# Two branches' gates and projections with tokens on the result's partitions, their sums transposed, and wide tiles moved by 128 bytes

## The chip, the core and the metric

The kernel runs on one core of one Trainium2 chip. The metric is device time in microseconds, from the first to the last instruction of a launch and what lies around it; lower is better. Before the change the median of three runs is 2205.89 us (2203.31 to 2206.0).

## What is computed

One residual block over 512 tokens of width 2048, in f32. The input is normalised and goes through one wide projection; its columns feed three branches and three merge gates:

```
conv_y = b_gate * conv3(c_gate * u);  o_conv = (conv_y * silu(conv_z)) @ w_conv_out     # 1024 -> 2048
mla_y  = latent attention, 16 heads;  o_mla  = (mla_y  * silu(mla_z))  @ w_mla_out      # 2048 -> 2048
mem_y  = attention to 256 tokens;     o_mem  = (mem_y  * silu(mem_z))  @ w_mem_out      # 1024 -> 2048
merged = sigmoid(g_conv)*o_conv + sigmoid(g_mla)*o_mla + sigmoid(g_mem)*o_mem
out    = x + merged @ w_o                                                               # 2048 -> 2048
```

## The kernel before

**A product of two f32 matrices** is three matmuls: each operand is split into a high part (rounded to float32r, ScalarE, line 122) and a rest (VectorE, line 124), and `mm3` (lines 150 to 155) adds high x high, high x rest and rest x high. Weights come from HBM in chunks of 128 x 1024 values (512 KB) into `raw` tiles, and each chunk is split into `whi` and `wlo` two chunks ahead of its use; there are three such pairs of buffers and ten `raw` tiles, of which the projections' split inputs take six.

**Block groups.** The big products (2048 x 2048 by 512 tokens) are done as a two-by-two block scheme with seven products instead of eight, P1 to P7 (line 913). Each takes a sum or difference of weight blocks (VectorE, `pre`, three chunks ahead) and a sum or difference of token blocks: `00`, `10`, `11`, and the forms T1 to T4, kept split in tiles `blk` (even), `hU` (odd) and `f` (forms), and made for eight pairs of channel blocks by `build` (line 1147) in four steps: sums, evens, forms, odds. The products land in four kinds of banks X, Y, Z, W.

- `block_group` (line 923) gives 512 output channels in 14 chunks. Channels lie on the result's partitions: the weights are the stationary operand, 256 tokens the moving one. A chunk is 24 matmuls 256 wide. It takes one PSUM bank for each of X, Y, Z, W, and groups alternate between the tags `aux` and `acc`, four banks each.
- `block_group_t` (line 1036) gives 1024 channels in 28 chunks with tokens on the result's partitions: token blocks are stationary, 512 weight columns move. A chunk is 12 matmuls 512 wide. It takes two banks for each of X, Y, Z, W, that is all eight. Only the output projection `w_o` (two groups, `out_group`, line 1616) uses it.

A *plain group* (`plain_group`, line 871) is an ordinary product, 24 matmuls 512 wide per chunk. `projection` (line 1474) runs four of them with their gates; before, all in mode F: weights stationary, 512 tokens moving.

**Order of the stages.** Memory keys and values (to 126 us), latent projections, 16 heads of attention with the memory queries' and gates' plain groups between and behind them (to 733 us), then 24 block groups: eight for the convolution's inputs, four for `mla_z`, then four each for the gates of memory, convolution and MLA (`gate_group`, line 1452). The gates go through a sigmoid to `gdram`. Then the memory's projection (16 chunks), multiplied by its gate and stored as first sums to `mdram`; four block groups of the MLA projection (`mla_group`, line 1542), which multiply by the gate, add the sums and store them again; the convolution's projection (16 chunks); and the two output groups.

**The order within.** `drive` (line 794) goes through the planned chunks; at each it emits loads that are due, `pre` and `prep` for later chunks, then small pieces of VectorE's and ScalarE's work (each with a due chunk, a cost and, with `by`, a chunk at which it is emitted in any case) as far as VectorE's room lets them, then the matmuls. Each engine works through its instructions in the order they are emitted. Loads go over SP's queue, stores over ScalarE's, adding transfers over POOL's.

**The junction.** In the convolution's projection a pair p of channel blocks (two blocks of 128) takes these steps, at chunks in the lists of lines 1578 and 1579: its gates are loaded (GATES), its sums are loaded (SUMS, `load_m`, line 1600), the product is multiplied by the gate (TIMES, line 1592), added to the sums (ADDS; for pairs 0 to 3 and 5 by an adding transfer, line 1587, else on VectorE, line 1589), and the four steps of `build` make the token blocks for `w_o` (FORMS). The first output group starts at chunk 16 in the order P1, P7, P5, P6 for each quarter of the pairs.

**Layout.** Wide tiles are allotted in whole multiples of 512 bytes (`Lines`, line 76), on the left side of SBUF from the end of a pool of small tiles, on the right side from the top. A fill of 48 floats (line 49) is in the small pool: with it every wide tile on the left (weights, `raw`, the projections' inputs, the identity) starts 128 bytes past a multiple of 512, and every one on the right (`blk`, `hU`, `f`) at a multiple.

Of the kernel before, what the change touches and what calls it, by code (L numbers as in the profile page):

```python
# [48 lines left out]
SMALL_FILL = 48  # L49
# [45 lines left out]
def body(ctx, tc, a, out):  # L95
# [16 lines left out]
    psum = ctx.enter_context(tc.tile_pool(name="ps", bufs=4, space=bass.MemoryType.PSUM))  # L112
# [3 lines left out]

    def bank(tag):
        return psum.tile([P, 512], F32, tag=tag, name=tag)
# [650 lines left out]


# [90 lines left out]
    tags = [0]  # L861

    def next_banks(n=4, tag=None):
        if tag is not None:
            tags[0] = ("aux", "acc").index(tag)
        else:
            tags[0] += 1
        return [bank("acc" if tags[0] % 2 else "aux") for _ in range(n)]


    def plain_group(src, nch, kc, n, xs, early=4, lead=2, tag=None):
# [4 lines left out]
        for c in range(nch):  # L876
# [13 lines left out]
            def mm(hold=hold, c=c):  # L890
                if c == 0:
                    banks.extend(next_banks(n // P, tag))
                hi, lo = hold["w"]
                for i in range(n // P):
                    for k in range(kc):
                        cols = slice(i * P, (i + 1) * P)
                        mm3(banks[i], (hi[:, k, cols], lo[:, k, cols]), xs(c * kc + k),
# [25 lines left out]
    def block_group(src, tokens, consume, loads=(-8, -7, -3, -2), add=None, halves=False):  # L923
# [70 lines left out]
        for n, ch in HALVES_ORDER if halves else PLAIN_ORDER:  # L994
# [22 lines left out]
                def mm(ch=ch, bn=bn, xn=xn, hold=hold):  # L1017
                    opens = bn not in bk
                    if not bk:
                        tags[0] += 1  # L1020
                        bk["tag"] = "acc" if tags[0] % 2 else "aux"
                    if opens:
                        bk[bn] = bank(bk["tag"])
# [12 lines left out]
    def block_group_t(src, tokens, results, tags_, early=6):  # L1036
# [10 lines left out]
        order = [(name, ch) for ch in range(4) for name in ("P1", "P7", "P5", "P6")]  # L1047
# [3 lines left out]
        for ch in range(4):  # L1051
            for b in range(3):
                when_raw(max(-3, first + max(4 * ch + b // 2 - early, -3 if early < 6 else -9)), 1, None,
                         lambda i=4 * b + ch: load(i))
            when_raw(first + 20 + 2 * ch - 6, 1, None, lambda i=12 + ch: load(i))
# [27 lines left out]
        for name, ch in order:  # L1083
# [21 lines left out]
            def mm(name=name, ch=ch, bn=bn, xn=xn, hold=hold):  # L1105
                opens = bn not in bk
                if opens:
                    bk[bn] = [bank(tags_["XYZW".index(bn)]) for _ in range(2)]
# [13 lines left out]
    def operands(b0, b1, f):  # L1122
        return {"00": (b0[:, 0, :HS], b0[:, 1, :HS]), "T1": (b0[:, 0, HS:], b0[:, 1, HS:]),
                "10": (b1[:, 0, :HS], b1[:, 1, :HS]), "11": (b1[:, 0, HS:], b1[:, 1, HS:]),
# [652 lines left out]
```

## Time and profile before

| | us |
|---|---|
| median of three runs | 2205.89 (2203.31 to 2206.0) |
| profiled execution, its own time | 2205.18 |
| its span, first to last instruction | 2203.4 |
| TensorE busy | 2149.7 |
| VectorE / ScalarE busy | 1575.1 / 1025.8 |
[...]

The span is what the rows below divide up; the profiled execution's own time is 1.8 us more. A matmul's printed duration holds its pipeline, so matmuls overlap; what one costs is the distance between starts.

### The profile page before, as it was taken

Reading aid. Unit: us, or ns where it says so; the run is one execution under the profiler, and the core shown is the slowest. Engines: PE = TensorE matmul, PEld = TensorE weight load, DVE = VectorE, ACT = ScalarE, POOL = GpSimd, SP = SyncE. Lnnn points to the kernel's source line nnn. Section 1 sums busy time; section 2 is a strip of 40 time slices with the busy share of each in tenths; the row PEclk is TensorE's granted clock in tenths of the full one; section 3 lists DMA queues with packets and bytes.
Section 4 is the critical chain, followed back from the end, with each engine's and each line's share of the span. In section 5 each row is a group of like instructions: output and inputs, shape, how many; then the busy total and the mean of one; then the engine's idle time right before and its main releaser. Section 6 shows DMA issues by size and latency. Waiting matters only on the chain.

```text
span 2203.4 us, 35901 instructions
## 1 busy us (share of the span) xinstructions
PE 2149.7 (98%) x14456; PEld 1981.4 (90%) x14456; DVE 1575.1 (71%) x2200; ACT 1025.8 (47%) x1547; POOL 171.8 (8%) x151
## 2 busy tenths in 40 slices
PE   7999999999999999999999999999999999999899
PEld 5788888898778999999999999999999899987787
DVE  7863777774335888787877777777676778857887
ACT  5532667774333444444444444444444443433433
POOL 6510311220001000000000000000000000000000
PEclk9999999999999999999999999999999999999999
DMA  7573212244228523333345334343344764577252
GB/s 260 154 257 107 87 55 67 76 143 147 76 77 258 191 90 106 131 101 124 112 170 185 130 115 149 125 146 125 114 147 149 253 215 164 183 240 253 78 206 91
DMA packets 115255, 322.61 MB, mean 146 GB/s; under 512 B 13200, under 2 KB 13456, under 8 KB 115088
## 3 DMA queue, kind: packets, MB, share of 16 engines
q1 hardware_dynamic: 90000, 274.87, 37.1%
q10 hardware_dynamic: 21600, 38.63, 4.7%
q0 software_dynamic: 3488, 6.82, 1.6%
q8 instruction: 113, 1.85, 0.3%
q14 instruction: 54, 0.44, 0.1%
HBM read 269.41 MB, written 48.23 MB: 144 GB/s over the span
## 4 chain that ended last, share of the span: by engine, by line
PE 68%; issue 2%; DVE 1%; ACT 0%; DMA 0%; POOL 0%; POOLq 0%; DVEq 0%; ACTq 0%
PE aux L155 11%; PE aux L153 11%; PE aux L154 11%; PE acc L154 11%; PE acc L153 11%; PE acc L155 11%; DVE wlo L124 0%; DMA eo<-y 0%; DVE raw L1096 0%; ACT whi L122 0%; DVE y L1592 0%; DVE f L124 0%; PE aux L204 0%; PE aux L1212 0%; DVE blk L124 0%
## 5 line engine op out<-in xcount | busy, mean ns | idle before, releaser
L124 DVE TENSOR_TENSOR wlo<-raw,whi 128x1024 fp32r<-128x1024 f32 x440 | 538.1, 1223 | 377.1 <-ACT whi L122 376.7
L122 ACT ACTIVATE whi<-raw 128x1024 fp32r<-128x1024 f32 x440 | 466.3, 1060 | 704.7 <-PE acc L154 297.6
L1007 DVE TENSOR_TENSOR raw<-raw 128x1024 f32<-128x1024 f32 x168 | 204.6, 1218 | 0.0
L155 PE MATMUL acc<-f,wlo 128*128 128x256 f32 x672 | 189.4, 282 | 0.0
L155 PE MATMUL aux<-f,wlo 128*128 128x256 f32 x672 | 189.4, 282 | 0.0
L154 PE MATMUL aux<-f,whi 128*128 128x256 f32 x672 | 189.3, 282 | 0.0
L154 PE MATMUL acc<-f,whi 128*128 128x256 f32 x672 | 189.3, 282 | 0.0
L153 PE MATMUL acc<-f,whi 128*128 128x256 f32 x672 | 189.1, 281 | 0.0
L153 PE MATMUL aux<-f,whi 128*128 128x256 f32 x672 | 189.1, 281 | 0.0
L147 DVE TENSOR_TENSOR wlo<-raw,whi 128x1024 fp32r<-128x1024 f32 (+3 forms) x97 | 117.7, 1215 | 96.0 <-ACT whi L146 94.7
L153 PE MATMUL acc<-blk,whi 128*128 128x256 f32 (+1 forms) x544 | 165.3, 304 | 9.0 <-ACT sq L1200 9.0
L154 PE MATMUL acc<-blk,whi 128*128 128x256 f32 (+1 forms) x544 | 164.2, 302 | 0.6 <-DVE blk L124 0.6
L154 PE MATMUL acc<-hU,whi 128*128 128x256 f32 (+1 forms) x544 | 164.1, 302 | 0.0
L153 PE MATMUL acc<-hU,whi 128*128 128x256 f32 (+1 forms) x544 | 164.1, 302 | 0.0
L155 PE MATMUL acc<-hU,wlo 128*128 128x256 f32 (+1 forms) x544 | 163.9, 302 | 0.0
L155 PE MATMUL acc<-blk,wlo 128*128 128x256 f32 (+1 forms) x544 | 163.7, 302 | 0.0
L146 ACT ACTIVATE whi<-raw 128x1024 fp32r<-128x1024 f32 (+3 forms) x97 | 92.6, 955 | 124.9 <-PE acc L155 49.2
L155 PE MATMUL aux<-blk,wlo 128*128 128x256 f32 (+1 forms) x480 | 138.9, 289 | 0.0
L155 PE MATMUL aux<-hU,wlo 128*128 128x256 f32 (+1 forms) x480 | 138.9, 289 | 0.0
L154 PE MATMUL aux<-hU,whi 128*128 128x256 f32 (+1 forms) x480 | 138.9, 289 | 0.0
L154 PE MATMUL aux<-blk,whi 128*128 128x256 f32 (+1 forms) x480 | 138.9, 289 | 0.0
L153 PE MATMUL aux<-hU,whi 128*128 128x256 f32 (+1 forms) x480 | 138.7, 289 | 0.0
(379 smaller groups left out, 5820.3 us busy)
## 6 DMA issues: line engine op xcount, KB each, us to landing
raw<-in_w_conv SPq DMA_DIRECT2D x64, 512.0 KB, 4.3
raw<-in_w_mlaz SPq DMA_DIRECT2D x32, 512.0 KB, 4.9
raw<-in_w_gmem SPq DMA_DIRECT2D x32, 512.0 KB, 4.2
raw<-in_w_gconv SPq DMA_DIRECT2D x32, 512.0 KB, 3.9
raw<-in_w_gmla SPq DMA_DIRECT2D x32, 512.0 KB, 3.7
raw<-in_w_mla_out SPq DMA_DIRECT2D x32, 512.0 KB, 5.2
raw<-in_w_o SPq DMA_DIRECT2D x32, 512.0 KB, 6.4
raw<-in_w_mem_kv SPq DMA_DIRECT2D x31, 512.0 KB, 3.6
```

The costliest lines, as they stand in the source:

```text
L122: act.activation(hi, src, AF.Copy, scale=1.0 if g is None else g)
L124: vec.tensor_tensor(out=lo, in0=src, in1=r32(hi), op=ALU.subtract)
L146: act.activation(hi[:, cols], raw[:, cols], AF.Copy)
L147: vec.tensor_tensor(out=lo[:, cols], in0=raw[:, cols], in1=r32(hi[:, cols]), op=ALU.subtract)
L153: nc.tensor.matmul(o, lhsT=s[0], rhs=m[0], start=start, stop=False, skip_group_check=shared)
L154: nc.tensor.matmul(o, lhsT=s[0], rhs=m[1], start=False, stop=False, skip_group_check=shared)
L155: nc.tensor.matmul(o, lhsT=s[1], rhs=m[0], start=False, stop=stop, skip_group_check=shared)
L1007: vec.tensor_tensor(out=o, in0=i0, in1=i1, op=op)
```

## The change

- The fill in the small pool goes from 48 to 16 floats. No other small tile changes, so every wide tile on the left starts 128 bytes earlier, at a multiple of 512.
- The gates of memory and of MLA and the MLA projection become two `block_group_t` each instead of four `block_group`; `gate_rows` and `mla_rows` take their results with tokens on partitions. The convolution's gates stay as they were and come first of the three.
- The memory's projection runs in mode T (tokens stationary, weights moving), so that gates and sums of two branches lie in `gdram` and `mdram` by tokens. The convolution's projection stays in mode F.
- The finished sums are therefore turned: `turn_sums` loads four row tiles for four channel blocks, transposes 16 blocks of 128 x 128 on TensorE into four banks, and ScalarE copies these to where the sums were loaded before. This is done four times, ahead of chunks 3, 7, 10 and 13 of the convolution's projection.
- All 16 products of that projection are added by transfers on POOL's queue. TIMES and FORMS of later pairs change.
- The first output group starts with P1 of three quarters, P7 of three, then P5 and P6 of three; the last quarter follows.
- Banks are handed out in four pairs, in rotation, instead of two tags of four.
- Loads of the y tiles in the MLA projection pass in order (`in_turn`). The odd block of `build` is allotted in its last step, and all forms are split in the third.

```diff
-SMALL_FILL = 48
+SMALL_FILL = 16
...
-    psum = ctx.enter_context(tc.tile_pool(name="ps", bufs=4, space=bass.MemoryType.PSUM))
+    psum = ctx.enter_context(tc.tile_pool(name="ps", bufs=2, space=bass.MemoryType.PSUM))
...
+    pairs = ["aux0", "aux1", "acc0", "acc1"]
+    def take_pairs(n):
+        t = pairs[:n]
+        pairs[:] = pairs[n:] + t
+        return t
...
-    def plain_group(src, nch, kc, n, xs, early=4, lead=2, tag=None):
+    def plain_group(src, nch, kc, n, xs, early=4, lead=2, tag=None, mode="F"):
...
+                        x, w = xs(c * kc + k), (hi[:, k], lo[:, k])
+                        s, m = (w, x) if mode == "F" else (x, w)
+                        mm3(banks[i], (s[0][:, cols], s[1][:, cols]), m,
...
-    def block_group_t(src, tokens, results, tags_, early=6):
+    def block_group_t(src, tokens, results, early=6, opening=()):
...
-        order = [(name, ch) for ch in range(4) for name in ("P1", "P7", "P5", "P6")]
+        order = list(opening)
+        order += [(name, ch) for ch in range(len(opening) // 4, 4) for name in ("P1", "P7", "P5", "P6")]
...
+                if not bk:
+                    bk["pairs"] = take_pairs(4)
+                    pairs[:] = [bk["pairs"][i] for i in (3, 1, 0, 2)]
...
-    for n, nm in enumerate(("w_gmem", "w_gconv", "w_gmla")):
-        for grp in range(4):
-            block_group(a[nm][grp], tx, gate_group(16 * n + 4 * grp))
+    for grp in range(4):
+        block_group(a["w_gconv"][grp], tx, gate_group(16 + 4 * grp))
+    for n, nm in ((0, "w_gmem"), (2, "w_gmla")):
+        for grp in range(2):
+            block_group_t(a[nm][grp], tx, gate_rows(16 * n, grp))
...
-    first = projection(a["w_mem_out"], 0, 0, mem_result)
+    first = projection(a["w_mem_out"], 0, 0, mem_result, mode="T")
...
-    for grp in range(4):
-        args = dict(loads=AFTER_PLAIN, halves=True) if grp == 0 else {}
-        block_group(a["w_mla_out"][grp], ta, mla_group(grp, len(plan)), **args)
+    for grp in range(2):
+        block_group_t(a["w_mla_out"][grp], ta, mla_rows(grp), 6 if grp else 5)
...
-    GATES, SUMS = (4, 4, 7, 7, 10, 12, 13, 14), (4, 4, 7, 7, 10, 11, 12, 13)
-    TIMES, ADDS, FORMS = (5, 5, 8, 8, 12, 12, 14, 16), (5, 5, 8, 8, 12, 12, 14, 16), (7, 7, 10, 10, 12, 14, 14, 16)
+    GATES = (4, 4, 7, 7, 10, 12, 13, 14)
+    TIMES, FORMS = (5, 5, 8, 8, 12, 12, 14, 16), (7, 7, 10, 10, 14, 14, 16, 20)
...
-            if p in (0, 1, 2, 3, 5):
-                nc.gpsimd.dma_start(out=m(), in_=sg(), accum_op=ALU.add)
-            else:
-                vec.tensor_tensor(out=m(), in0=m(), in1=sg(), op=ALU.add)
+            nc.gpsimd.dma_start(out=m(), in_=sg(), accum_op=ALU.add)
...
+    ASKED, TURNED = (0, 3, 7, 11), (3, 7, 10, 13)
+    def turn_sums(n):
+        hold, bs = [], []
+        def ask():
+            for i in range(2):
+                t = r32(f_tile(2 * n + i))
+                for q in range(2):
+                    v = t[:, q].rearrange("p a t -> p (a t)")[:, :S]
+                    nc.sync.dma_start(v, mdram[4 * n + 2 * i + q])
+                    hold.append(v)
+        def turn():
+            spot = 1 if n == 3 else 0
+            for f in range(4):
+                b = bank_of(pairs[spot + f // 2])
+                for i in range(NTB):
+                    nc.tensor.transpose(out=b[:, i * P:(i + 1) * P], in_=hold[i][:, f * P:(f + 1) * P], identity=ident)
+                bs.append(b)
+                later(0, 0, piece(lambda f=f: copy(f), by=first + TURNED[n]))
+        def copy(f):
...
+            act.activation(ms[p][:, f % 2], bs[f], AF.Copy)
+        at[first + ASKED[n]].append(ask)
+        phases[first + TURNED[n]].append(turn)
...
+        opening = [(name, ch) for names in (("P1",), ("P7",), ("P5", "P6")) for ch in range(3) for name in names]
+        block_group_t(a["w_o"][grp], to, results, early, () if grp else opening)
```

## Rows read from the trace of the kernel before

**Rows 1.** The page: busy time of each engine over the span, and the shares of the chain that ended last, by engine and by line.

```profile
PE 2149.7 (98%) x14456; PEld 1981.4 (90%) x14456; DVE 1575.1 (71%) x2200; ACT 1025.8 (47%) x1547; POOL 171.8 (8%) x151
...
PE 68%; issue 2%; DVE 1%; ACT 0%; DMA 0%; POOL 0%; POOLq 0%; DVEq 0%; ACTq 0%
```

**Rows 2.** Busy time by stage. Columns: the stretch in us from the start, its length, then busy us and instructions of PE, PEld (weight loads), DVE, ACT, POOL, then the granted clock, DMA's share and GB/s. The stretches: memory keys; attention; the last plain groups; 24 block groups; the memory's projection; the MLA projection; the convolution's projection; the junction; the rest of the output groups.

```profile
0.00:126.00 126.00, 103.75 (x427) 78.56 (x428) 100.39 (x102) 68.91 (x104) 75.46 (x48) 0.97 0.63 206
...
235.00:663.00 428.00, 411.26 (x2235) 355.76 (x2234) 264.03 (x736) 254.80 (x599) 72.49 (x77) 1.00 0.27 90
663.00:732.80 69.80, 69.80 (x302) 56.27 (x301) 43.22 (x72) 26.09 (x40) 10.80 (x12) 1.00 0.86 271
732.80:1690.80 958.00, 957.41 (x8065) 957.04 (x8065) 733.12 (x716) 440.01 (x499) 0.00 (x0) 1.00 0.38 128
1690.80:1777.80 87.00, 87.00 (x386) 72.03 (x385) 64.76 (x104) 37.39 (x57) 0.00 (x0) 1.00 0.79 281
1777.80:1939.10 161.30, 161.30 (x1346) 161.26 (x1345) 129.33 (x134) 66.32 (x70) 0.00 (x0) 1.00 0.50 169
1939.10:2026.20 87.10, 87.10 (x387) 72.13 (x386) 56.55 (x86) 29.07 (x41) 8.92 (x10) 1.00 0.81 253
2026.20:2080.00 53.80, 43.46 (x163) 33.38 (x162) 45.18 (x57) 21.44 (x27) 0.00 (x0) 0.87 0.40 137
2080.00:2199.20 119.20, 119.20 (x513) 95.89 (x511) 93.25 (x96) 46.67 (x49) 0.00 (x0) 1.00 0.40 137
```

**Rows 3.** TensorE in order of time: start in us, duration, line, what is written and read, width. Neighbouring matmuls of a block group (256 wide), of the convolution's projection and of an output group (512 wide).

```profile
1660.10 0.28 PE L155 MATMUL aux<-f,wlo 128*128 128x256 f32 x1
1660.22 0.28 PE L153 MATMUL aux<-f,whi 128*128 128x256 f32 x1
...
1999.97 0.39 PE L154 MATMUL acc<-act,whi 128*128 128x512 f32 x1
2000.20 0.39 PE L155 MATMUL acc<-act,wlo 128*128 128x512 f32 x1
...
2143.43 0.39 PE L153 MATMUL aux<-whi,blk 128*128 128x512 f32 x1
2143.65 0.40 PE L154 MATMUL aux<-wlo,blk 128*128 128x512 f32 x1
2143.89 0.39 PE L155 MATMUL aux<-whi,blk 128*128 128x512 f32 x1
```

**Rows 4.** What TensorE waited for over the whole span, those that fall in the junction: engine, tile and line, what it waited for, us in total, times, longest.

```profile
PE acc L153 <- ACT blk L122: 3.5, 1, 3.5
PE aux L153 <- ACT whi L122: 3.1, 1, 3.1
PE acc L153 <- DVE y L1592: 2.4, 1, 2.4
PE aux L154 <- DVE wlo L124: 1.3, 1, 1.3
```

**Rows 5.** TensorE in order of time in the junction; in brackets the idle time before an instruction and what ended it.

```profile
2035.40 0.63 PE L153 MATMUL aux<-whi,f 128*128 128x512 f32 x1
2035.83 0.63 PE L154 MATMUL aux<-wlo,f 128*128 128x512 f32 x1
...
2038.45 0.40 PE L155 MATMUL aux<-whi,f 128*128 128x512 f32 x1
2041.29 0.66 PE L153 MATMUL acc<-whi,blk 128*128 128x512 f32 x1 [2.45 <-DVE y L1592]
```

**Rows 6.** VectorE and POOL in order of time in the junction: pair 5's two products, its two adding transfers, its first sum, and pair 7's first sum.

```profile
2018.84 1.28 DVE L1592 TENSOR_TENSOR y<-acc,y 128x512 f32<-128x512 f32 x2
...
2020.13 1.77 POOL L1587 DMA_DIRECT2D eo<-y  x2 [23.63 <-issue]
...
2027.75 0.42 DVE L1154 TENSOR_TENSOR t<-eo 128x256 f32<-128x256 f32 x1 [1.77 <-DMA eo<-y]
...
2073.61 0.41 DVE L1154 TENSOR_TENSOR t<-eo 128x256 f32<-128x256 f32 x1
```

**Rows 7.** DMA issues of the page: what is loaded, queue, count, size of one, median us from issue to landing.

```profile
raw<-in_w_mla_out SPq DMA_DIRECT2D x32, 512.0 KB, 5.2
raw<-in_w_ukv SPq DMA_DIRECT2D x16, 512.0 KB, 3.5
raw<-in_w_memq SPq DMA_DIRECT2D x16, 512.0 KB, 5.0
raw<-in_w_memz SPq DMA_DIRECT2D x16, 512.0 KB, 3.6
eo<-mdram SPq DMA_DIRECT2D x16, 256.0 KB, 5.2
eo<-y POOLq DMA_DIRECT2D x10, 256.0 KB, 5.4
```

**Rows 8.** Transposes of attention in order of time (four per row), and groups of ScalarE's and VectorE's instructions of the late stages (count, busy us, mean ns of one, idle before): a bank copied by ScalarE, and the additions of pairs 4, 6 and 7.

```profile
294.54 0.63 PE L204 MATMUL aux<-ident,qn 128*128 128x128 f32 x4
295.01 0.60 PE L204 MATMUL aux<-ident,qd 128*128 128x128 f32 x4
...
L945 ACT ACTIVATE u<-aux 128x512 f32<-128x512 f32 x2 | 1.2, 582 | 0.0
L1589 DVE TENSOR_TENSOR eo<-eo,y 128x512 f32<-128x512 f32 x6 | 4.2, 692 | 0.2
```

More of the change, by code (lines that the diff above doesn't have):

```diff
@@ L1459, in gate_group, with rows, gate_rows, results @@
         return consume
+    def rows(j, name, tb):
+        return 4 * (2 * j + int(name[0])) + 2 * int(name[1]) + tb
+    def gate_rows(n0, grp):
+        first = len(plan)
+        def results(name, o, i0, i1):
+            ts = {}
+            def made(tb):
+                if o is not None:
+                    vec.tensor_tensor(out=o(tb), in0=i0(tb), in1=i1(tb), op=ALU.add) if i0 is not None else None
+                    ts[tb] = o(tb)
+                    return
+                used["y"] += 1
+                ts[tb] = pres.tile([P, S], F32, tag="y", name="gy", bufs=4)
+                if i1 is None:
+                    act.activation(ts[tb], i0(tb), AF.Sigmoid)
+                else:
+                    vec.tensor_tensor(out=ts[tb], in0=i0(tb), in1=i1(tb), op=ALU.add)
+            def sigmoid(tb):
+                act.activation(ts[tb], ts[tb], AF.Sigmoid)
+            def store(tb):
+                nc.scalar.dma_start(gdram[n0 + rows(grp, name, tb)], ts[tb])
+                if o is None:
+                    freed("y")
+                elif tb:
+                    freed({"11": "r1", "01": "r0"}[name])
+            out_ = [(0, 0 if i1 is None else 0.69, piece(lambda tb=tb: made(tb), by=first + 29)) for tb in range(2)]
+            if not (o is None and i1 is None):
+                out_ += [(1, 0, lambda tb=tb: sigmoid(tb)) for tb in range(2)]
+            return out_ + [(2, 0, lambda tb=tb: store(tb)) for tb in range(2)]
+        return results
     AFTER_PLAIN = (-3, -2, -1, 0)
@@ L1500, in group @@
         def group(src, nch, kc, n, j):
-            g0, banks = plain_group(src, nch, kc, n, lambda k: acts[k], early=3)
+            g0, banks = plain_group(src, nch, kc, n, lambda k: acts[k], early=3, mode=mode)
             sgs = []
@@ L1568, in body, with load @@
-    for grp in range(4):
-        args = dict(loads=AFTER_PLAIN, halves=True) if grp == 0 else {}
-        block_group(a["w_mla_out"][grp], ta, mla_group(grp, len(plan)), **args)
+        def load(name, tb, k):
+            ys[name, tb, k] = y_tile((mdram if k else gdram[32:])[rows(grp, name, tb)])
+        in_turn("y", [(first + c, lambda name=name, tb=tb, k=k: load(name, tb, k))
+                      for c, name in ((12, "11"), (16, "10"), (20, "00"), (24, "01"))
+                      for k in range(2) for tb in range(2)])
@@ L1610, in body, with out_group @@
     conv_first = first = len(plan)
     projection(a["w_conv_out"], 8, 16, conv_result, a["w_conv_last"], GATES)
-    for p in range(8):
-        when(first + SUMS[p], "r1" if p == 7 else "m", lambda p=p: load_m(p))
-    def out_group(grp, tags_, early):
+    for n in range(4):
+        turn_sums(n)
+    def out_group(grp, early):
         first = len(plan)
```

163 lines of the change are left out of this document (91 added, 72 removed).

## The prediction

> **What bounds the kernel now.** I read the page's busy shares first, then a table of stages, then the start times of single matmuls, and last TensorE's waits. TensorE is busy 98% of the span, and its own rows lead the chain that ended last [rows 1]; VectorE is at 71%, so the question is what a matmul costs. In the table [rows 2] the reader is to see three things. From 732.8 to 1939.1 us PE is busy without a break, and so is PEld: 957.04 of 958.00 us. Where the moving operand is 256 wide, loading weights fills the whole time, so a 256-column matmul cannot come faster than its weight load. Where it is 512 wide, PEld falls to 72 of 87 us and the matmul itself is the limit. The one later place where PE is not full is 2026.2 to 2080.0, behind the convolution's projection.
>
> The spacing of starts gives the prices. 256 columns: 958.0 us over 8,064 matmuls (24 groups of 336), 118.8 ns, and 161.3 over 1,344 in the MLA projection, 120.0 [rows 2, 3]. 512 columns have two prices: in the projections 87.0/384 = 226.6 ns, in the output groups 119.2/513 = 232.4, in the last plain groups 69.8/300 = 232.7 [rows 2, 3]. The duration printed beside a matmul (0.28, 0.39) includes pipeline and is not the price.
>
> Why two? In the program's layout left-hand tiles (weights, activations of the projections) start 128 bytes past a multiple of 512, right-hand ones (blocks, forms) at a multiple. A projection reads both operands at the same remainder and pays 226.6; an output group reads weights at 128 and blocks at 0 and pays 232.4; the plain groups have the roles swapped and pay 232.7. I take it that unequal remainders cost 5.8 ns on 512 columns.
>
> **The parts and their cost.** The sum is made against the profiled execution, 2205.2 us (span 2203.4), 0.7 below the median of the runs, which lie between 2203.3 and 2206.0.
>
> *Gates of memory and MLA.* 112 chunks leave the 256-wide routine: 2,688 matmuls x 118.8 ns = 319.3 us become 1,344 at 512. With the 128 bytes out of the small pool, weights (left) and blocks (right) are both at remainder 0; priced as the other equal pair, 226.6 ns, that is 304.5: **-14.8**. Upper end 232.4 ns (312.3): -7.0. Products, weight differences, splits and evictions keep their number and width; VectorE's 85% at most is not the bound (below).
>
> *MLA projection.* 161.3 us become 672 x 226.6 = 152.3: **-9.0**; at 232.4, -5.1. VectorE has 129.33 of 161.30 us there [rows 2], the same work in 152.3 is 85%, and ScalarE 66; both stay beside PE. The 32 loads of gates and sums per stage keep their number but pass the four y tiles in turn; a load that waits for a tile holds the weight loads behind it on SP's queue. Weight loads are asked some six chunks (16 us) ahead against 5.2 us to landing [rows 7], so I cost that at 0, up to +5 if this cover goes.
>
> *Output groups.* The same 672 matmuls go from 232.4 to 226.6: **-3.9** (0 to -4.5).
>
> *Earlier wide matmuls.* The 16 + 16 + 16 chunks of w_ukv, w_memq and w_memz [rows 7] are 24 wide matmuls each, 1,152 x 6.1 ns = 7.0 us. PE is busy 411.26 of 428.00 us and then 69.80 of 69.80 there [rows 2], so most comes through: **-5** (0 to -7). The memory keys' stage, PE 103.75 of 126.00, waits for others: 0 (to -2).
>
> *Memory projection* turned to tokens on partitions: same count and width, both operands on the left: 0. Its results reach the sums' rows through the same 16 stores.
>
> *Transposes.* 64 new ones, four per bank in 16 banks. Four take 0.47 us from start to start [rows 8]: **+7.5**, on PE's path, since PE has no gaps there. Below: 0 is excluded, as PE is full in that stage (87.10 of 87.10). Their 16 evictions on ScalarE at 0.58 us [rows 8] are 9 us in a stage where it is busy 29.07 of 87.10: hidden. Their 16 loads are as many as the loads of sums they replace, asked 2 to 4 chunks of 5.4 us ahead, against 5.2 us [rows 7]. Above: 16 in a row with nothing else between are in no row here. [...]
>
> *The junction.* 53.8 us hold 163 matmuls, 37.9 us at 232.4 ns: 15.9 us are lost today [rows 2]. Four waits, 10.3 us [rows 4], and after each some eight matmuls at half clock [rows 5]. Their origins: (a) pair 5's products run at 2018.84, its accumulating transfer is issued at 2020.13 and lands 7 us later, and VectorE stands until 2027.75 [rows 6] with P7's weight difference and split queued behind; (b) P5 opens a bank that VectorE has not yet emptied (2041.29 [rows 5]); (c) P1's fourth chunk wants pair 7's block, begun at 2073.61 [rows 6]. The change takes pair 5's products one chunk earlier (six vector additions, 4.2 us [rows 8], become transfers) and moves P5 and P6 to the seventh and eighth chunk: (b) goes, some 4 us. On (a) I am cautious: forms of pairs 4 and 5 now both stand at chunk 14, with pair 6's products, about 13 us of VectorE in two chunks of 5.4, and P1's second and third chunk want their split right behind. (c) stays: the order reaches pair 7's block by force at the same chunk. With POOL, 16 issues of 0.89 us instead of 10; its queue has nothing else. New wait: pair 6's and 7's sums now wait for a transfer of 5.4 us [rows 7] too, behind which VectorE's next splits queue; they have two and four chunks (10.9 us) for it. I take 10 lost of 15.9: **-6** (-16 to +6).
>
> Sum: -14.8 - 9.0 - 3.9 - 5 + 7.5 - 6 = -31.2, **2174 us**. The bounds added alone on each side give about 2157 and 2207; they do not all fall together.
>
> **The rivals.** *The 128 bytes buy nothing.* Today form and address go together: every wide group with tokens on partitions has unequal remainders and every projection equal ones, so the 232.4 could belong to the form. Then -7.0 - 5.1 + 0 + 0 + 7.5 - 6 = -10.6, 2195. If instead remainder 0 is the bad one, the 768 wide matmuls of the two projections, now at 226.6, rise by 5.8 ns, 4.5 us: 2199. For it: only one equal pair (128, 128) is in the rows. Against: both unequal orders cost the same, whichever operand is at 0. [...] Chance 0.14.
>
> *The junction is not mended*: the VectorE burst at chunks 14 to 16 takes the place of the stalls. 2180 with nothing gained, 2186 with six lost. For it: VectorE has 45.18 of 53.8 us there now. Chance 0.16.
>
> *Slower: the eight banks.* A wide group holds all of PSUM (two banks each for X, Y, Z, W), so P5 and P6 of the next open banks that P2 and P3 of the last filled two or three chunks ago. The price of one such wait is in the rows: 2038.45 to 2041.29, 2.6 us idle, and eight matmuls at 0.43, 1.6 us: 4.2. Six new groups with two each would be 12 x 4.2 = 50 us, 2224. It decides from nine waits on (8 x 4.2 = 34 only takes back the 31). Against: the second output group opens in the same way between 2080 and 2199.2, and PE is busy all 119.20 us [rows 2]. Chance 0.07.
>
> **How the numbers follow.** The forecast, 2174, has 0.63, its own range 2160 to 2188 by the junction's and the early stage's ends. With the second rival and the lower half of the first, 2160 to 2197 holds about 8 in 10. A measurement here can tell about 0.2%, 4.4 us, from no change, so faster is below 2201.5: 0.63 + 0.16 + most of 0.14, less the tails, 0.88; the same 0.05; slower 0.07.
>
> **What would show it.** Right: starts 227 ns apart in gates, MLA projection, output groups and in the last plain groups; PEld below PE there; no PE wait at openings of wide groups; transposes 16 x 0.47 us inside the convolution's projection; one or two waits with a half clock behind the projection, P5's gone. Wrong: starts 232 ns apart (first rival), 239 or 232 in the projections, waits on evictions at each group's third chunk (third rival), a granted clock under 1.00 after transposes, or PE waiting for y tiles in the MLA projection.

## The result, and the profile after

The changed kernel takes 2212.68 us (median of nine runs, 2208.95 to 2215.9) against 2205.89 for the kernel before on the same chip: 1.0034 times as long, 95% interval 1.0024 to 1.0045. The forecast was 2174 in a range up to 2197, so it was wrong, by 39 us and in sign. The profiled execution took 2208.95 us, its span is 2207.2. It is the fastest of the nine, so the stages below account for 35 us of the 39; the other 4 stand in no trace.

By stage (columns as in [rows 2]: stretch and length, busy us of PE, PEld, DVE, ACT and POOL, granted clock, DMA share, GB/s). The stretches: attention; last plain groups; convolution's inputs; `mla_z`; gates of memory and MLA; memory's projection; MLA projection; convolution's projection; start and rest of the output groups.

```profile
235.00:663.00 428.00, 404.52 (x2199) 352.37 (x2198) 261.00 (x731) 252.72 (x589) 75.48 (x76) 0.99 0.26 90
663.00:735.30 72.30, 72.30 (x324) 59.95 (x323) 44.40 (x77) 28.19 (x44) 10.73 (x12) 1.00 0.83 262
735.30:1058.70 323.40, 322.81 (x2689) 322.58 (x2688) 258.71 (x264) 143.52 (x161) 0.00 (x0) 1.00 0.34 115
1058.70:1220.00 161.30, 161.30 (x1346) 161.30 (x1345) 125.91 (x126) 73.58 (x83) 0.00 (x0) 1.00 0.44 154
...
1381.30:1686.00 304.70, 304.70 (x1347) 252.29 (x1346) 231.06 (x215) 145.28 (x163) 0.00 (x0) 1.00 0.39 130
1686.00:1773.00 87.00, 87.00 (x386) 72.03 (x385) 64.41 (x104) 36.52 (x56) 0.00 (x0) 1.00 0.76 267
1773.00:1931.40 158.40, 153.85 (x674) 125.61 (x673) 128.81 (x133) 63.33 (x65) 0.00 (x0) 1.00 0.50 170
1931.40:2039.00 107.60, 100.26 (x450) 81.63 (x449) 55.76 (x86) 39.44 (x59) 10.70 (x12) 0.95 0.77 244
2039.00:2092.00 53.00, 45.46 (x184) 36.14 (x183) 45.48 (x56) 24.53 (x33) 3.53 (x4) 0.94 0.39 118
2092.00:2207.00 115.00, 111.05 (x490) 91.60 (x489) 91.49 (x95) 42.92 (x43) 0.00 (x0) 1.00 0.43 147
```

Set beside the kernel before (from the first start of a stage to that of the next, differences taken before rounding; in the last column 0 stands where a part had no term):

| stage | before | after | difference | forecast |
|---|---|---|---|---|
| up to the first block group | 732.9 | 735.3 | +2.5 | -5 |
| 16 block groups that stay 256 wide | 639.0 | 646.0 | +7.0 | 0 |
| gates of memory and MLA | 319.0 | 304.7 | -14.3 | -14.8 |
| memory's projection | 87.1 | 87.0 | 0 | 0 |
| MLA projection | 161.3 | 158.4 | -2.9 | -9.0 |
| convolution's projection | 87.1 | 107.6 | +20.5 | +7.5 |
| output groups | 177.1 | 168.2 | -8.9 | -9.9 |
| sum | | | +3.8 | -31.2 |

The gates, as wide groups, came as forecast; 34 of the 35 us are in four other rows (7.5, 7.0, 6.1 and 13.0). TensorE's prices, as in [rows 3], are now 227 ns from start to start where 512 columns move, and 120 in place of 118.8 where 256 do. Two neighbouring matmuls at the start of the first block group, and two of a wide gate group:

```profile
735.32 0.28 PE L160 MATMUL acc<-blk,whi 128*128 128x256 f32 x1
735.43 0.28 PE L161 MATMUL acc<-blk,whi 128*128 128x256 f32 x1
...
1499.63 0.39 PE L160 MATMUL aux<-whi,f 128*128 128x512 f32 x1
1499.86 0.39 PE L161 MATMUL aux<-wlo,f 128*128 128x512 f32 x1
```

What TensorE waited for from 1730 to 2110 us, the five largest (us in total, times, longest; splits are lines 129 and 131, the products of the memory's projection with its gate 1598). Of the waits of [rows 4], the one for pair 7's block is still there, and longer; those for split activations and for products in banks ahead of wide groups are new.

```profile
PE acc L160 <- ACT blk L129: 5.3, 1, 5.3
PE acc L161 <- DVE act L131: 3.6, 2, 2.2
PE acc L160 <- ACT act L129: 3.3, 2, 1.8
PE aux L160 <- DVE y L1598: 3.1, 1, 3.1
PE acc L161 <- DVE wlo L131: 1.5, 1, 1.5
```

The largest loss lies where the convolution's projection opens. In order of time, TensorE, then SP's queue, ScalarE and VectorE there (start, duration; in brackets the idle time before and what ended it):

```profile
1936.58 0.39 PE L162 MATMUL acc<-act,wlo 128*128 128x512 f32 x1
1938.81 0.50 PE L160 MATMUL acc<-act,whi 128*128 128x512 f32 x1 [1.84 <-ACT act L129]
1941.48 0.79 PE L161 MATMUL acc<-act,whi 128*128 128x512 f32 x1 [2.17 <-DVE act L131]
1942.07 0.63 PE L162 MATMUL acc<-act,wlo 128*128 128x512 f32 x1
1942.50 0.63 PE L160 MATMUL acc<-act,whi 128*128 128x512 f32 x1
```

```profile
1921.66 2.38 SPq L1214 DMA_DIRECT2D y<-gdram  x2
1924.09 0.43 SPq L903 DMA_DIRECT2D raw<-in_w_conv_out  x1
...
1930.89 2.13 SPq L1214 DMA_DIRECT2D y<-mdram  x2
1933.12 0.38 SPq L903 DMA_DIRECT2D raw<-in_w_conv_out  x1
```

```profile
1937.18 1.06 ACT L129 ACTIVATE whi<-raw 128x1024 fp32r<-128x1024 f32 x1 [3.04 <-DMA raw<-in_w_conv_out]
1938.15 1.14 ACT L129 ACTIVATE act<-araw 128x512 fp32r<-128x512 f32 x2
```

```profile
1938.27 1.23 DVE L131 TENSOR_TENSOR wlo<-raw,whi 128x1024 fp32r<-128x1024 f32 x1 [1.54 <-ACT whi L129]
...
1940.13 0.69 DVE L1641 TENSOR_TENSOR y<-y 128x512 f32<-128x512 f32 x1
1940.74 1.29 DVE L131 TENSOR_TENSOR act<-araw,act 128x512 fp32r<-128x512 f32 x2
```

Read from below: VectorE splits the second pair of activations at 1940.74, behind products and sums of the MLA projection; ScalarE did so at 1938.15, behind a weight split that stood 3.04 us for its load; that load left SP's queue at 1933.12, behind the loads of two sums (1930.89) that wanted y tiles, the four buffers into which gates and sums are loaded. Y tiles come free when VectorE has used them, so the three queues hold each other (from 1885 to 1970 us SP's loads of y tiles stand 8.0 us for VectorE's sums of line 1641); VectorE itself stands 2.73 us ahead of 1934.17 and 1.54 ahead of 1938.27 for weight splits. Behind these waits the granted clock is 0.50 from 1940.3 to 1947.1 us, with 0.43 us from start to start in place of 0.227; behind the waits at 1951 it is 0.50 again, from 1954.0 to 1957.4 (0.95 over the stage). By distances from start to start the two openings cost 12.3 of the stage's 20.5 us more, 6.8 and 5.5; the four batches of transposes, with a wait of 0.4 us ahead of the last and the slower starts just behind each, cost the other 8.3.

### The profile page after: what moved, and what is told of

The parts are those of the page before. It is cut to its first block, busy times and chain, and to the rows that moved or that the text cites. A ratio compares the mean times of both kernels' runs of the same rounds, so it can differ in the third digit from the quotient of the medians.

```text
span 2207.2 us, 31861 instructions
## 1 busy us (share of the span) xinstructions
PE 2138.1 (97%) x12504; PEld 1896.5 (86%) x12504; DVE 1574.5 (71%) x2194; ACT 1031.1 (47%) x1551; POOL 181.3 (8%) x157
## 4 chain that ended last, share of the span: by engine, by line
PE 88%; DVE 5%; DMA 2%; ACT 2%; issue 2%; POOL 1%; ACTq 0%; SPq 0%; DVEq 0%; POOLq 0%
PE acc L161 16%; PE acc L160 16%; PE acc L162 16%; PE aux L161 12%; PE aux L160 12%; PE aux L162 12%; DVE wlo L154 1%; PE aux L211 1%; DVE wlo L131 1%; PE aux L667 1%; DMA raw<-in_w_conv_out 1%; ACT whi L129 1%; POOL xs L311 1%; PE aux L647 0%; PE aux L649 0%
## 5 line engine op out<-in xcount | busy, mean ns | idle before, releaser
L160 PE MATMUL acc<-whi,blk 128*128 128x512 f32 (+1 forms) x320 | 120.7, 381 | 7.3 <-ACT blk L129 5.3
L161 PE MATMUL acc<-wlo,blk 128*128 128x512 f32 (+1 forms) x320 | 119.7, 375 | 2.4 <-DVE wlo L131 1.5
L160 PE MATMUL acc<-blk,whi 128*128 128x256 f32 (+1 forms) x352 | 112.1, 319 | 8.0 <-ACT sq L1231 8.0
L162 PE MATMUL acc<-whi,blk 128*128 128x512 f32 (+1 forms) x320 | 119.3, 374 | 0.0
L160 PE MATMUL acc<-whi,f 128*128 128x512 f32 x288 | 112.6, 391 | 0.5 <-DVE u L1631 0.5
L161 PE MATMUL acc<-wlo,f 128*128 128x512 f32 x288 | 112.6, 391 | 0.0
L162 PE MATMUL acc<-whi,f 128*128 128x512 f32 x288 | 112.4, 390 | 0.0
L161 PE MATMUL acc<-blk,whi 128*128 128x256 f32 (+1 forms) x352 | 111.3, 316 | 0.6 <-DVE blk L131 0.6
L129 ACT ACTIVATE whi<-s 128x1024 fp32r<-128x1024 f32 x64 | 67.9, 1061 | 93.8 <-PE aux L161 21.1
L162 PE MATMUL acc<-blk,wlo 128*128 128x256 f32 (+1 forms) x352 | 110.5, 315 | 0.0
L160 PE MATMUL acc<-hU,whi 128*128 128x256 f32 (+1 forms) x352 | 110.0, 312 | 0.0
L161 PE MATMUL acc<-hU,whi 128*128 128x256 f32 (+1 forms) x352 | 109.8, 312 | 0.0
L162 PE MATMUL acc<-hU,wlo 128*128 128x256 f32 (+1 forms) x352 | 109.5, 312 | 0.0
L160 PE MATMUL acc<-f,whi 128*128 128x256 f32 x384 | 108.7, 283 | 0.0
L161 PE MATMUL acc<-f,whi 128*128 128x256 f32 x384 | 108.7, 283 | 0.0
```

The source lines that it names most:

```text
L129: act.activation(hi, src, AF.Copy, scale=1.0 if g is None else g)
L160: nc.tensor.matmul(o, lhsT=s[0], rhs=m[0], start=start, stop=False, skip_group_check=shared)
L161: nc.tensor.matmul(o, lhsT=s[0], rhs=m[1], start=False, stop=False, skip_group_check=shared)
L162: nc.tensor.matmul(o, lhsT=s[1], rhs=m[0], start=False, stop=stop, skip_group_check=shared)
```

## The experiments

Times are medians; ratios are to the kernel before on the same chip, with their 95% intervals. A stage in one profiled execution varies: the first block group starts between 735.3 and 738.1 us in five kernels whose order up to there is that of the changed kernel, and the output groups take 167.1 to 170.9 us in five kernels whose edits lie elsewhere (the changed kernel, `a_tags`, `a_prod`, `a_ypool`, `a_accum`).

**The layout: the 128 bytes alone, and all but them.**

```diff
-SMALL_FILL = 48        # b_shift: the kernel before with 16
+SMALL_FILL = 16
...
-SMALL_FILL = 16        # a_noshift: the changed kernel with 48
+SMALL_FILL = 48
```

> The kernel before with one number changed: the fill of 16 in place of 48 floats, nothing else. Theory A (a price goes with the two operands' addresses modulo 512): starts in the two output groups fall from 232.4 to 226.7 ns (672 matmuls, -3.9 us) and in the last plain groups from 232.7 to 227 (with the earlier wide stages -5 us, so that the first block group starts at about 728); the 8,064 matmuls 256 wide, whose two operands now both lie at a multiple of 512, rise from 118.8 to 120.0 ns, +10 us, which the plan for the change left out. Together about +1 us: about 2206, ratio 1.000 to 1.001. Rival B (the price belongs to the form of the group, not to the address): output groups stay at 232.4, block groups at 118.8, first block group at 732.9, time 2205 to 2206. The two give the same time and differ in the starts of each stage.

> The changed kernel with the fill of 48 floats put back, nothing else. Theory A (addresses): the 16 groups that stay 256 wide fall from 120.0 to 118.8 ns (5,376 x 1.25 ns = -6.7 us); the wide groups with tokens stationary rise from 226.7 to 232.4 ns (gates 1,344, MLA projection 672, output groups 672: 2,688 x 5.8 = +15.6 us) and the earlier wide groups by 5 to 7: about 2226, ratio 1.006. Rival B (the form): no stage moves by more than 1 us, about 2212.

Measured: `b_shift` 2207.95 us, 1.0019 (1.0010 to 1.0029); first block group at 727.63, block groups at 120.0 ns (24 groups, +10.6 us), output groups 174.0 in place of 177.1. `a_noshift` 2227.39, 1.0106 (1.0088 to 1.0124). Against the changed kernel, its 16 narrow groups take 7.0 us less; gates +7.6, MLA projection +4.9, the convolution's projection +2.2, output groups +2.7, and the early stages +7.4. Theory A, the address, holds in both directions; rival B, the form of the group, fell. So the shift gives some 25 us in the changed kernel and takes 7 back, in the narrow groups, a stage that the forecast gave no term (17.9 net between the two profiled executions). Gates of memory and MLA in `a_noshift`, to be read against 304.70 above:

```profile
1381.70:1694.00 312.30, 312.30 (x1347) 253.19 (x1346) 231.14 (x215) 145.35 (x163) 0.00 (x0) 1.00 0.37 127
```

**The layout: which property of the address.** The kernel before with fills of 80 and 112 floats: 256 and 384 bytes past a multiple of 512.

> The kernel before with a fill of 80 floats: every wide tile on the left starts 256 bytes past a multiple of 512 (0 in the shifted kernel, 128 in the kernel before), those on the right at a multiple. Theory A1 (equal remainders by 512 are what counts): unequal, so all is as before: output groups 232.4 ns, block groups 118.8, first block group at 732.9, time 2205. Theory A2 (equal remainders by 256 count): as in the shifted kernel: output groups 226.7, block groups 120.0, first block group at 727.6, time 2208.

> The kernel before with a fill of 112 floats: the left tiles start 384 bytes past a multiple of 512. Theories A1 and A2: unequal, as before (232.4, 118.8, 732.9, 2205). Rival U (only a distance of exactly 128 bytes costs, or the price changes with the distance): other prices, 226.7 or above 232.4.

Measured: `b_fill80` 2207.7 us, 1.0010 (0.9999 to 1.0021), output groups 174.0 us, first block group at 725.6; `b_fill112` 2204.97, 0.9993 (0.9981 to 1.0006), output groups 176.8, first block group at 733.0. A stretch of 500 us that holds nothing but matmuls 256 wide, in `b_shift` (0), `b_fill80` (256), the kernel before (128) and `b_fill112` (384); the first number in brackets is that of the matmuls that PE runs in it, the second that of the weight loads:

```profile
1100.00:1600.00 500.00, 500.00 (x4169) 500.00 (x4168) 365.31 (x348) 230.84 (x263) 0.00 (x0) 1.00 0.41 139
```

```profile
1100.00:1600.00 500.00, 500.00 (x4169) 500.00 (x4169) 365.74 (x350) 230.35 (x263) 0.00 (x0) 1.00 0.40 138
```

```profile
1100.00:1600.00 500.00, 500.00 (x4216) 500.00 (x4215) 370.69 (x354) 232.10 (x265) 0.00 (x0) 1.00 0.41 140
```

```profile
1100.00:1600.00 500.00, 500.00 (x4216) 500.00 (x4215) 370.64 (x353) 232.01 (x265) 0.00 (x0) 1.00 0.41 140
```

So 0 and 256 behave alike, and 128 and 384: A2, the remainder by 256. Equal remainders give 226.7 ns at 512 columns and 120.0 at 256, unequal ones 232.4 and 118.7 (the 118.8 of the rows holds the slow first matmuls too). The projections, whose two operands both lie on the left, stay at 226.7 under all four fills (before, the memory's projection takes 87.0 us for 384, and `b_fill112` has the same 5,822 matmuls from 1051.1 to 1783.3 us; in `b_shift` these 732.2 us are 5,376 x 120.0 ns and 384 x 226.7, with 5,762 matmuls, and `b_fill80` has 5,763), so what counted in these four layouts is that the remainders are equal, and not which they are. The weight loads (PEld) fill the stretch at either price, 500.00 of 500.00 us. The 256-wide price holds for the gates and inputs; the MLA projection at 256 wide is at 120.0 in the kernel before and in `b_shift` alike (161.3 us for 1,344 in both), which no run here explains. The starts are not alike, though: in the kernel before they go some 118, 120 and 122 ns in turn in the MLA projection, and from 115 to 122 in the gates and inputs; in the changed kernel's narrow groups each distance is 120 ns.

**The early stages: how banks are handed out.**

```diff
-    psum = ctx.enter_context(tc.tile_pool(name="ps", bufs=4, ...))    # b_pairs, from before
+    psum = ctx.enter_context(tc.tile_pool(name="ps", bufs=2, ...))
...
-    def bank(tag):
-        return psum.tile([P, 512], F32, tag=tag, name=tag)
+    def bank(tag, turns=defaultdict(int)):
+        turns[tag] += 1; return psum.tile([P, 512], F32, tag=f"{tag}{turns[tag] % 2}", name=tag)
...
-    psum = ctx.enter_context(tc.tile_pool(name="ps", bufs=2, ...))    # a_tags, from after
+    psum = ctx.enter_context(tc.tile_pool(name="ps", bufs=4, ...))
...
-        return psum.tile([P, 512], F32, tag=tag, name=tag)
+        return psum.tile([P, 512], F32, tag=tag[:3], name=tag[:3])
```

> The kernel before with its PSUM pool in four tags of two banks, handed out in turn, in place of two tags of four; the fill stays at 48 floats. Of the change only the way of handing out the banks in the stages up to 733 us is in it. Theory C (attention's loss comes from the banks): the first block group starts at 739 to 741 in place of 732.9 (the wide groups stay at 232.7 ns, so the 5 to 7 us that the shift gives back are not there), total about 2212. Rival D (the loss comes with the shift, or from elsewhere): it starts at 732 to 734, total about 2206.

> The changed kernel with PSUM again in two tags of four banks, so that TensorE's order up to 733 us is that of the kernel before; the shift of 128 bytes stays, and every group asks for banks in the same order of tags as now. Theory C (the early loss is the banks' handing out): the first block group starts at about 728, as in the kernel before with the shift alone (727.6), against 735.3; -7, about 2205, if the wide groups' openings don't wait. Rival M (tags of four hand the wide groups a bank still in use): the start is 728, but openings in gates, MLA projection and output groups wait some 4 us each, and the time is 2212 or more.

Measured: `b_pairs` 2215.76 us, 1.0050 (1.0034 to 1.0066), first block group at 739.10; `a_tags` 2203.46, 0.9993 (0.9982 to 1.0003), at 728.98 against 735.3, with the later stages within 1.3 us. Theory C holds, M fell. (`b_pairs` is 11 us slower by its ratio; its profiled execution, the fastest of four, shows 6.6, of which 6.2 lie ahead of the first block group.) TensorE's waits between 235 and 600 us, `b_pairs`, then `a_tags` (L204 and L211 are the same line in the two, the transposes of attention's heads; `ptl` are split probabilities, and the wait for them is that of a transpose for a bank that VectorE still reads):

```profile
PE aux L204 <- DVE ptl L124: 5.9, 4, 2.0
...
PE aux L660 <- ACT s L653: 1.5, 1, 1.5
```

```profile
PE aux L211 <- DVE ptl L131: 0.9, 1, 0.9
```

With two tags of two in turn, attention's transposes and scores run in another order, and the longer waits of that stretch add up to 18.8 us against 11.2 in the kernel before, where the wait for `ptl` is 0.9. Whether the order or the bank that each gets does it was not separated.

**The MLA projection's opening.** `a_prod`, from after:

```diff
-        return [(0, 0.69, piece(lambda: vec.tensor_tensor(out=sg(), in0=b(), in1=sg(), op=ALU.mult), sg)),
+        return [(0, 0.69, piece(lambda: vec.tensor_tensor(out=sg(), in0=b(), in1=sg(), op=ALU.mult), sg,
+                                **(dict(by=len(plan)) if j >= 12 else {}))),
```

> The changed kernel with the last four products of the memory's projection emitted at the MLA projection's first chunk in any case. Theory I (TensorE's 3.1 us wait at the opening of the MLA projection is for banks that VectorE empties late, since the products stand behind two weight differences and two splits): that wait and the 0.4 us ahead of it go, with the half clock behind; MLA projection 158.4 to about 154, time -4: 2208. Rival J (VectorE has no room there): a weight split is late in place of the bank, and the stage stays within 1 us of 158.4.

Measured: 2206.56 us, 1.0001 (0.9986 to 1.0015). The stage falls from 158.4 to 153.9 us, PE is busy all but 0.9 of it, and both waits for line 1598 are gone: theory I. There was no half clock to win back: the granted clock of the stage is 1.00 with the waits, too (from 1773.0 to 1931.4 us of the changed kernel).

```profile
1774.10:1928.00 153.90, 153.00 (x673) 125.87 (x673) 129.21 (x133) 63.32 (x65) 0.00 (x0) 1.00 0.51 177
```

**The opening of the convolution's projection.** `a_ypool` moves the y loads of the MLA projection to POOL's queue; `a_accum` replaces the 16 loads of the sums and their 16 additions by transfers, so it takes work from VectorE and loads from SP's queue at once:

```diff
-            ys[name, tb, k] = y_tile((mdram if k else gdram[32:])[rows(grp, name, tb)])              # a_ypool
+            ys[name, tb, k] = y_tile((mdram if k else gdram[32:])[rows(grp, name, tb)], nc.gpsimd)
...
-                      for k in range(2) for tb in range(2)])                                          # a_accum
+                      for k in range(1) for tb in range(2)])
...
-                    vec.tensor_tensor(out=t, in0=t, in1=ys[name, tb, 1], op=ALU.add)
-                    freed("y")
+                    nc.gpsimd.dma_start(out=t, in_=mdram[rows(grp, name, tb)], accum_op=ALU.add)
...
-            return out_ + [(3, 0, lambda tb=tb: store(tb)) for tb in range(2)]
+            return out_ + [(5, 0, lambda tb=tb: store(tb)) for tb in range(2)]
```

> The changed kernel with the gate and sum loads of the MLA projection (the four y tiles) on POOL's queue instead of SP's; nothing else moves. Theory E (a load that waits for a free y tile holds the loads of activations and weights of the convolution's projection behind it on SP's queue): the convolution's projection falls from 107.6 to about 96 us, because its first two chunks no longer wait for split inputs; about -11 us in all, 2201, ratio to the changed kernel 0.995. Rival F (VectorE's backlog from the MLA projection, or a bank emptied late, is what TensorE waits for): the stage stays at 106 to 108 us and the time at 2212.

> The changed kernel, but in the MLA projection the stored sums are added by 16 transfers on POOL's queue, in place of 16 loads into y tiles on SP's and 16 additions on VectorE (the same way as in the convolution's projection); the store comes two chunks later. Theory G (VectorE, with the results of 1,024 channels all due at a group's end and its queue standing for y tiles, splits the activations of the convolution's projection late): 16 x 0.69 = 11 us of VectorE and half of the y loads are gone, eight of each in the group just ahead of the convolution's projection; that projection falls from 107.6 to about 96 us and the MLA projection by 1 to 3; about 2200, ratio to the changed kernel 0.994. Rival H (the weights and activations are loaded late because raw tiles come free late, whatever VectorE does with the sums): the projection stays above 104 us, time 2209 to 2213.

Measured: `a_ypool` 2214.61 us, 1.0053 (1.0034 to 1.0073): the stage stays at 106.5 us and the MLA projection takes 160.7, so E by itself fell. The weight loads stand there for VectorE instead, which is busy from 1919.6 to 1934.8 us but for 0.6, and empties their raw tiles late. What the loads of line 903 (the projection's weights) waited for on SP's queue from 1885 to 1970 us, in the changed kernel, then in `a_ypool`:

```profile
SPq L903 <- DVE wlo L131: 7.4, 5, 2.8
```

```profile
SPq L903 <- DVE wlo L131: 26.3, 7, 6.6
```

`a_accum` 2202.72, 0.9986 (0.9973 to 1.0000): the stage falls to 100.1 us, not to 96, and the MLA projection rises to 161.0; G holds for the larger part, though this run does not part VectorE's additions from the loads that went with them. ScalarE's waits from 1915 to 1960 us for late data, `a_ypool`, then `a_accum`:

```profile
ACT whi L129 <- DMA raw<-in_w_conv_out: 13.0, 4, 5.3
ACT whi L129 <- DVE raw L1121: 5.6, 2, 3.2
```

```profile
ACT whi L129 <- DMA raw<-in_w_conv_out: 6.3, 2, 4.5
ACT whi L129 <- DMA mdram<-y: 2.3, 1, 2.3
```

**The output groups.** `a_forms`, from after:

```diff
-        need = conv_first + 16 + 4 * (p // 2)
+        need = conv_first + (16 + 4 * (p // 2), 24, 25)[max(0, p - 5)]
```

> The changed kernel with the token blocks of pairs 6 and 7 emitted at the latest at chunks 24 and 25 of the junction's count, four and three chunks earlier than now. Theory K (TensorE's 5.7 us wait at P1's fourth chunk is only the plan's due time for pair 7's block): the wait goes, and with it some 3 us of half clock; output groups 168.2 to 160 to 162, time -6 to -8: 2205. Rival L (VectorE is full there; the forced work makes weight splits late instead): output groups stay above 166.

Measured: 2209.57 us, 1.0020 (1.0010 to 1.0029); output groups 165.2 us. The 5.3 us wait for pair 7's block is gone (theory K), but two weight splits behind the forced work are late in its place, with 1.28 and 1.31 us idle at 2080.8 and 2082.6 (rival L). The stage is 3.0 us shorter, half of the expected gain at most, and not much more than it varies by; the time's interval overlaps that of the changed kernel.

**All four, and what was left.**

```diff
-                nc.scalar.dma_start(mdram[rows(grp, name, tb)], ...)             # a_all_q, from a_all
+                nc.gpsimd.dma_start(mdram[rows(grp, name, tb)], ...)
-                at[first + (-2, -1, 1, 2)[c]].append(                            # a_all_e, from a_all_q
+                at[first + (-2, -2, 0, 1)[c]].append(
-            ys[name, tb, k] = y_tile((mdram if k else gdram[32:])[rows(grp, name, tb)])              # a_all_p, from a_all_e
+            ys[name, tb, k] = y_tile((mdram if k else gdram[32:])[rows(grp, name, tb)], nc.gpsimd)
```

> The changed kernel with the four edits of the last group together: PSUM in two tags of four, the last four products of the memory's projection forced, the MLA projection's sums added by transfers, pair 6's and 7's token blocks forced at chunks 24 and 25. If the four causes are separate (theory N), their stage gains add: attention -6.3, MLA projection -4.5 (+2.5 from the transfers' version), convolution's projection -7.4, output groups -2.9; about 2193, ratio to the kernel before 0.994. Rival O (one backlog of VectorE and of SP's queue, pushed from stage to stage): the total stays at 2200 or more.

> As the one before it, but the MLA projection's stores go out on POOL's queue, behind the adding transfers that they wait for. Theory P (a store on ScalarE's queue that waits for its adding transfer holds the weight split behind it, 2.3 us once ahead of the convolution's projection): 2 to 4 us less than the one before it, in the MLA projection and the opening of the next. Rival Q (ScalarE waits for late weights there anyway): no difference above 1 us.

> As the one before it, and the splits of the projections' second to fourth pair of activations are planned one chunk earlier. Theory R (the activations' splits of the convolution's projection stand on ScalarE and VectorE behind a weight split that waits for its load): they come ahead of it, and the convolution's projection falls from about 100 to 96 to 97 us; -3 us. Rival S (the activations themselves are loaded late): no difference.

> As the one before it, and the gate loads of the MLA projection go over POOL's queue. Theory E again, now with VectorE's backlog taken away (a gate load that waits for a y tile holds the weight load behind it on SP's queue): the last of TensorE's waits at the opening of the convolution's projection goes, 1 to 3 us less. Rival T (on POOL the gate loads stand behind stores that wait for adding transfers, and VectorE waits for gates in place of weights): 1 to 4 us more.

| | us | ratio (interval) | first block group at | MLA projection | convolution's | output groups |
|---|---|---|---|---|---|---|
| `a_all` | 2185.65 | 0.9910 (0.9892 to 0.9928) | 728.6 | 154.8 | 99.8 | 164.5 |
| `a_all_q` | 2188.41 | 0.9920 (0.9904 to 0.9936) | 729.6 | 153.8 | 103.9 | 161.7 |
| `a_all_e` | 2187.09 | 0.9913 (0.9894 to 0.9932) | 727.4 | 153.8 | 99.5 | 167.0 |
| `a_all_p` | 2184.48 | 0.9902 (0.9885 to 0.9919) | 729.2 | 153.8 | 95.3 | 164.5 |

The four gains add (N), to somewhat more than was expected (2193): `a_all` beats both kernels, by 0.9% and 1.2%. The span of `a_all` is 21.8 us below that of the changed kernel, and the four stages differ by 6.7 + 3.5 + 7.8 + 3.7. The intervals of all four versions overlap, so the three later ones are told apart by their stages alone, of one profiled execution each. P fell (`a_all_q`: 1 us less in the MLA projection, 4 more in the next, 3 less in the output groups). R takes 4.4 us from the convolution's projection of the version ahead of it, but the output groups give 5.3 back, so it is not shown to gain. E, which did nothing while VectorE was late, takes another 4.2 from the projection and 2.5 from the output groups: in `a_all_p` TensorE waits for nothing at that opening. Stages of `a_all_p` (the convolution's projection, the output groups), one batch of transposes, and TensorE's two largest waits from 1730 to 2110 us:

```profile
1920.60:2015.90 95.30, 94.86 (x449) 78.75 (x449) 52.61 (x81) 38.19 (x58) 16.55 (x21) 1.00 0.85 266
2015.90:2180.40 164.50, 154.46 (x673) 125.56 (x672) 136.97 (x152) 67.19 (x75) 3.54 (x4) 1.00 0.42 141
```

```profile
1936.97 1.91 PE L1706 MATMUL aux<-ident,f 128*128 128x128 f32 x16
1938.63 0.48 PE L160 MATMUL acc<-act,whi 128*128 128x512 f32 x1
```

```profile
PE acc L161 <- DVE wlo L131: 3.7, 3, 1.6
PE acc L160 <- ACT whi L129: 2.2, 2, 1.5
```

## Why the prediction was wrong

*Right.* Gates of memory and MLA: -14.3 for -14.8, at 227 ns a start. Output groups and junction: -8.9 for -9.9; the wait (b) went and (c) stayed, as argued. That the junction's term came so near is in part luck: (c) grew from 3.5 to 5.3 us, and the waits for weight splits, on which the prediction was cautious, fell from 4.4 to 2.2. Memory's projection: 0. Transposes: three batches of 1.67 us and one of 2.2 behind a wait, 7.2 together, for 7.5. The rows held no 16 together; in the changed kernel the granted clock falls to 0.50 at 1940.3 and 1954.0 us, behind the waits of the two openings and ahead of the first batch (1960), and is 1.00 over the 3 us behind each of the four batches; `a_all_p` has 1.00 over the whole stage that holds them. No longer run of transposes was tried.

*The rival on the 128 bytes.* Addresses it is: `b_shift` moves no form and has the lower wide price, 226.7 ns in place of 232.4; its output groups take 174.0 us in place of 177.1.

*Wrong, in the prediction's own steps:*

1. **"a 256-column matmul cannot come faster than its weight load"**, with PEld as full as PE, was taken as a price that no address moves, so the narrow groups that stay had no term. The same shift raises them from 118.7 to 120.0 ns: 5,376 x 1.3 = +7.0, as seen. PEld fills the time at either price (500.00 of 500.00 us in `b_shift` and before), so a full PEld did not say what the price was. The rows held a sign of it: 118.8 in one stage and 120.0 in another, both quoted and not asked about.
2. **Earlier wide matmuls, -5.** The term is right (`b_shift` starts its first block group 5.2 us earlier). What had no term was the line of the change on banks: only the wide groups were looked at for it, but attention uses the same pool, and loses 6.2 us by it (`b_pairs`; 6.3 in `a_tags`). With 1.3 more, which lies within what this stage varies by, that is the row's 7.5.
3. **MLA projection, -9.0.** The matmuls' price came true (672 x 226.7 = 152.3). The stage has 6.1 us of waits and of slower starts behind them, at a granted clock of 1.00, and `a_prod` gives 4.5 back: the rival of the eight banks, in its place, but once at full size in place of twelve times, and in a product of the stage ahead that had no forced chunk.
4. **Loads of the y tiles: "0, up to +5 if this cover goes".** The cover went, one stage later than looked for, and 12.3 us were lost at the two openings. The prediction added up VectorE's work over the stage (85%) and did not ask when it falls due: a wide group's results come at its end, 1,024 channels at once, and the splits of the next stage's activations queue behind them. Taking the 16 additions away, with their 16 loads, gives 7.4 us (`a_accum`). SP's queue, the mechanism that was named, is worth nothing while VectorE is late (`a_ypool`) and 4.2 us of this stage when it is not (`a_all_p`); how the 7.4 part between additions and loads is not shown.

Each was an edit or a stage costed at nothing, or, with the bank wait, given to a rival that stood or fell as a whole. So the chance of a slower kernel, 0.07, was one mechanism's where four small ones together made 34 of the 35 us. A sum hid it, too: the bounds "about 2157 and 2207" leave out one of the prediction's own upper ends, the y tiles' +5. With it the parts give about 2159 and 2212 for the profiled execution, which took 2208.95 and so lies inside.

*Open.* Why the narrow price goes the other way with the remainder; why the MLA projection's narrow groups were at 120.0 before the shift, too; what in attention's order makes the 6 us; and why the median of the changed kernel lies 3.7 us above its profiled execution.

## What to carry to other kernels

A change of a shared constant (a fill, a pool's tags) is priced in every stage that uses it, not in the one it is made for: here 7.0 us in the narrow groups for the fill, 6.2 ahead of them for the tags. Fewer and larger groups took 14.3 us off the gates here, but they bring their results at one moment, and 12.3 us were lost at the two openings: count what the vector engine must do between a group's last matmul and the next stage's first operands, and what loads wait behind tiles that this work frees. A queue that looks guilty in the trace may only be the next in line; removing one of two waits in series may show little until the other is gone (`a_ypool` 106.5 us for 107.6, the same edit in `a_all_p` 95.3 for 99.5).

## What the runs showed of the hardware

In these runs a float32r matmul's price went with whether both operands start at the same remainder by 256 bytes. At 512 columns it was 226.7 ns if so and 232.4 if not (output groups 174.0 us in `b_shift` and `b_fill80`, 177.1 before and 176.8 in `b_fill112`). At 256 columns it was the other way round, 120.0 and 118.7, in gates and inputs (4,169 matmuls in 500 us in `b_shift` and `b_fill80`, 4,216 before and in `b_fill112`), but 120.0 in the MLA projection both before and in `b_shift`. Sixteen 128 x 128 transposes in a row took 1.67 us between wide matmuls in the changed kernel, and the granted clock was 1.00 over the 3 us behind them, as over the whole stage in `a_all_p`.
